# Seven-product form for the last eight hidden tiles of the second down projection, with sums of eight weight blocks made ahead

## The chip, the cores and the metric

The kernel runs on one core of one Trainium2 chip. The metric is the device time of one execution in microseconds (us), as the median of three runs. The engines of a core work side by side: TensorE (PE in the profile, its weight loads as PEld), VectorE (DVE), ScalarE (ACT), GpSimd (POOL), and SyncE (SP), whose queue issues nearly all transfers of this kernel.

## The reference

One layer of a diffusion backbone on 512 latent tokens and 256 context tokens of width 1024, all in float32: a half-step SwiGLU feed-forward stage, a token mixer (latent attention and a gated MLP, side by side), and a second half-step feed-forward stage. Each stage is modulated by a condition vector. The parts that matter here:

```python
def swiglu(h, w1, w3, w2):
    return (jax.nn.silu(h @ w1) * (h @ w3)) @ w2      # D_MODEL 1024, D_FF 2816

x = ffn_sublayer(x, ..., ffn1_w1, ffn1_w3, ffn1_w2)   # latent; the context likewise
proj = modulate(rms_norm(x, norm2_w), ...) @ w_in     # input projection of the mixer
x = x + mx[5] * token_mix(...)
x = ffn_sublayer(x, mx[6], mx[7], mx[8], norm3_w, ffn2_w1, ffn2_w3, ffn2_w2)   # returns x
```

The output is the latent stream, 512 x 1024.

## The kernel before

**Layout.** Activations lie with the channels on the 128 partitions and the tokens along the free dimension. The 2816 hidden channels of a feed-forward stage are 22 tiles of 128 (f = 0 to 21), the 1024 model channels are 8 tiles (dt or k).

**Precision.** Every float32 operand is held as a pair of rounded tensors, high and low: ACT casts the high part (`oph`, `gh`), DVE subtracts it from the source for the low part (`opl`, `gl`). A product is three matmuls: high by high, high by low, low by high (`mm3`). `Stream.operand` makes such a pair from 512 columns of a loaded weight.

**Second feed-forward stage, up.** Tiles 0 to 3 are done plainly. From tile 4 on, class `Winograd` treats tile f of w1 and w3, four channel tiles in and 256 + 256 tokens as a two by two block product, in seven block products instead of eight (Strassen's scheme in Winograd's form). One product (`prod`) is 12 matmuls of 128 x 128 by 256 columns. The weight block of a tile is one load of 1 MB (`block`, four parts of 512 columns); four sums of these parts are made by four POOL instructions per tile (`prep`, `block_sums`, `third`; results in `s` or in place). So a tile needs seven pairs, four of them from sums. The seven products run in an order that allows tile f + 1 to be opened before tile f ends (`open`, `unit`); the evacuations of PSUM are short generators that `Flow.slot` plays between products.

**Second feed-forward stage, down.** `CHUNKS2 = [4, 4, 4, 4, 2, 4]`: after units 4, 8, 12, 16 and 18 `down_flow` multiplies the last four, four, four, four or two finished hidden tiles with their part of w2, for each of the eight dt over all 512 tokens (matmuls of 512 columns), and adds the result to `x` by one DVE instruction per dt (`evac_lat`). The last four tiles are multiplied behind all units by `down`, which also sends each finished row of `x` to the output.

**What sets the order.** In the stages around the change each engine's instructions are kept in the order in which the program records them. `Flow` is a queue of weight pairs: it makes up to `OPS` = 5 pairs ahead of the product that uses them, during `down_flow` up to `OPS + MORE` = 9. SP issues loads in its own fixed order; a load waits there until its buffer is free, and everything behind it waits too. There are three buffers for loads of 512 KB (`raw`) and two for 1 MB (`block`), besides one in the pool `third`.

**End of the first stage and the input projection.** `last_mm(g, dt)` is the last down projection of the first stage, for the two halves g of the tokens, 16 calls of 18 matmuls. `last_ev` adds the result to `x` and squares it; `SsqAcc` sums the squares on DVE (`sqa`), splits the sum (`sqh`, `sql`) and has PE add it over the partitions (`done_split`). `norm2(g)` makes the normalised operand (`hf`, then `hh` and `hl`) for `in_k(g, k)`, the input projection, eight steps for each half. Behind it `uv_unit` and `QTile` follow: the gated MLP's projections and the query tiles, whose weights come through `raw`. `turned` and the `QTile`s share two PSUM buffers (`big`). POOL's first work there is `kpT` (a memset) and `rk`, powers needed by the queries.

## Time and profile before

| | us |
|---|---|
| median of 3 runs | 1104.32 (1104.23 to 1104.5) |
| time of the profiled execution | 1104.5 |
| its span, first to last instruction | 1102.5 |
| PE busy | 1097.5 |
| DVE busy | 892.8 |
| ACT busy | 536.5 |
| POOL busy | 310.3 |

The profiled execution took 2.0 us more than its span, and 0.2 us more than the median. PE is busy through nearly the whole span; the granted TensorE clock is 1.0. POOL works in bursts: in the two feed-forward stages it makes the weight sums, between 474 and 538 us of the span it has nothing to do. The rows on which the prediction rests stand in it. In a row of the timeline the first number is the start in the span, the second the duration; in a row of groups the last pair before the bar's end is busy time and mean ns of one.

### The profile page before, as it was taken

The numbers are of one execution on the slowest core, as the hardware profiler recorded it, in microseconds if no ns is written. First come the engines' busy times: TensorE is split into PE (matmuls) and PEld (weight loads), VectorE is DVE, ScalarE is ACT, GpSimd is POOL, SyncE is SP. The second block draws the span as 40 slices with busy tenths as digits, with TensorE's granted clock in tenths as the row PEclk, the third lists the DMA queues.
The fourth block names the chain that finished last, engine by engine and source line by source line (L and its number), as shares of the span: only waits on it lengthen the run. The fifth ranks groups of instructions, "written<-read, shape, count | busy, mean of one in ns | idle before, by whom it ended". The sixth has DMA issues, their size and how long they took to land.

```text
span 1102.5 us, 19621 instructions
## 1 busy us (share of the span) xinstructions
PE 1097.5 (100%) x7610; PEld 1052.5 (95%) x7610; DVE 892.8 (81%) x1594; ACT 536.5 (49%) x1115; POOL 310.3 (28%) x269
## 2 busy tenths in 40 slices
PE   9999999999999999999999999999999999999998
PEld 7899999999999999999998889999999989898997
DVE  5779998888878769866867899989988878787883
ACT  6545422431344214443765549986663535354450
POOL 0003303311344013400009317860014444352420
PEclk9999999999999999999999999999999999999999
DMA  9721354234334664412241310103222322424202
GB/s 354 279 60 47 120 172 139 100 137 148 106 124 151 233 201 164 149 54 93 97 132 61 102 50 21 39 21 102 91 94 89 123 78 93 137 78 132 99 21 77
DMA packets 35677, 125.95 MB, mean 114 GB/s; under 512 B 3712, under 2 KB 10624, under 8 KB 30976
## 3 DMA queue, kind: packets, MB, share of 16 engines
q1 hardware_dynamic: 35440, 124.63, 33.2%
q8 instruction: 60, 0.98, 0.4%
q14 instruction: 33, 0.27, 0.1%
q10 hardware_dynamic: 144, 0.06, 0.1%
HBM read 122.58 MB, written 2.10 MB: 113 GB/s over the span
## 4 chain that ended last, share of the span: by engine, by line
PE 96%; DMA 1%; DVE 1%; ACT 1%; POOL 0%; issue 0%; SPq 0%; ACTq 0%; POOLq 0%; DVEq 0%
PE mm L60 61%; PE one L60 20%; PE big L60 10%; PE big L616 1%; PE mm L601 1%; DMA scale<-wada 1%; PE mm L177 1%; PE mm L176 1%; PE mm L178 1%; PE mm L338 1%; DMA x<-xT 0%; PE big L608 0%; DVE sq L60 0%; POOL pe L60 0%; ACT hh L60 0%
## 5 line engine op out<-in xcount | busy, mean ns | idle before, releaser
L60 DVE TENSOR_TENSOR opl<-block,oph 128x512 fp32r<-128x512 f32 x216 | 195.4, 912 | 32.6 <-ACT oph L60 29.9
L60 POOL TENSOR_TENSOR block<-block 128x512 f32<-128x512 f32 x69 | 105.0, 1522 | 378.9 <-DVE opl L60 376.2
L60 ACT CAST oph<-block 128x512 fp32r<-128x512 f32 x216 | 132.3, 622 | 108.8 <-PE mm L60 85.5
L60 PE MATMUL mm<-gl,oph 128*128 128x256 f32 (+2 forms) x573 | 176.4, 308 | 0.0
L60 PE MATMUL mm<-gh,opl 128*128 128x256 f32 (+2 forms) x573 | 176.4, 308 | 0.0
L60 PE MATMUL mm<-gh,oph 128*128 128x256 f32 (+2 forms) x573 | 176.4, 308 | 0.0
L60 PEld LDWEIGHTS mm<-gh,oph 128*128 128x128 f32 x573 | 107.6, 188 | 5.5
L60 PEld LDWEIGHTS mm<-gh,opl 128*128 128x128 f32 x573 | 107.6, 188 | 5.4
L60 PEld LDWEIGHTS mm<-gl,oph 128*128 128x128 f32 x573 | 107.6, 188 | 5.4
L60 ACT CAST oph<-raw 128x512 fp32r<-128x512 f32 x127 | 76.0, 620 | 69.7 <-PE mm L60 44.4
L60 DVE SCALAR_TENSOR_TENSOR x<-mm,g,x 128x512 f32<-128x512 f32 (+2 forms) x136 | 78.7, 600 | 28.5 <-PE mm L60 27.9
L60 DVE TENSOR_TENSOR opl<-raw,oph 128x512 fp32r<-128x512 f32 x127 | 88.1, 710 | 15.3 <-ACT oph L60 14.0
L60 POOL TENSOR_TENSOR block<-s,block 128x512 f32<-128x512 f32 x35 | 48.3, 1379 | 123.8 <-DVE opl L60 122.3
L60 PE MATMUL mm<-hh,oph 128*128 128x384 f32 (+2 forms) x195 | 64.9, 333 | 0.0
L60 PE MATMUL mm<-hl,oph 128*128 128x384 f32 (+2 forms) x195 | 64.8, 333 | 0.0
L60 PE MATMUL mm<-hh,opl 128*128 128x384 f32 (+2 forms) x195 | 64.8, 333 | 0.0
L60 DVE SCALAR_TENSOR_TENSOR junk<-raw,cb 128x1024 bf16<-128x1024 f32 x48 | 62.1, 1308 | 0.2 <-DMA raw<-wada 0.2
L60 POOL TENSOR_TENSOR s<-block 128x512 f32<-128x512 f32 x34 | 53.7, 1579 | 11.4 <-DMA block<-wst 11.4
L60 DVE SCALAR_TENSOR_TENSOR raw<-raw,cb 128x1024 f32<-128x1024 f32 x32 | 42.1, 1322 | 8.3 <-DMA raw<-wada 8.2
L60 PE MATMUL one<-hl,oph 128*128 128x384 f32 x144 | 48.1, 334 | 0.0
L60 PE MATMUL one<-hh,oph 128*128 128x384 f32 x144 | 48.1, 334 | 0.0
L60 PE MATMUL one<-hh,opl 128*128 128x384 f32 x144 | 48.1, 334 | 0.0
(699 smaller groups left out, 3361.9 us busy)
## 6 DMA issues: line engine op xcount, KB each, us to landing
raw<-wst SPq DMA_DIRECT2D x77, 512.0 KB, 3.8
block<-wst SPq DMA_DIRECT2D x36, 1024.0 KB, 4.9
raw<-wada SPq DMA_DIRECT2D x56, 512.0 KB, 4.3
scale<-wada SPq DMA_DIRECT2D x16, 512.0 KB, 9.0
x<-xT SPq DMA_DIRECT2D x5, 512.0 KB, 6.4
raw<-wfirst SPq DMA_DIRECT2D x8, 256.0 KB, 8.8
out<-x SPq DMA_DIRECT2D x7, 256.0 KB, 2.3
raw<-wuq SPq DMA_DIRECT2D x2, 384.0 KB, 5.1
```

The costliest lines, as they stand in the source:

```text
L60: return lambda *a, **k: self.tc.keep_in_program_order(f(*a, **k))
L176: nc.tensor.matmul(out, lh, rh, start=first, stop=False, skip_group_check=more)
L177: nc.tensor.matmul(out, lh, rl, start=False, stop=False, skip_group_check=more)
L178: nc.tensor.matmul(out, ll, rh, start=False, stop=last, skip_group_check=more)
L338: pin(nc.tensor.matmul(pa[q, :P], scw[:, kt, 2 - 2 * w : 34 - 2 * w], units[d][w][:, kt * P : kt * P + P], start=w == 0 and kt < 4, stop=w ...
L601: pin(nc.tensor.matmul(o, l[:, c], r, start=k == 0 and m == 0 and w == 0, stop=k == NK - 1 and m == 2, skip_group_check=True))
L616: pin(nc.tensor.matmul(two(pbs[i]), ops[k][lo][:, i * P : i * P + P], lat(r, k), start=False, stop=k == NK - 1 and m == 2, skip_group_chec ...
```

## The change

**Down projection of tiles 14 to 21.** `CHUNKS2` becomes `[4, 4, 4, 2]`, so `down_flow` runs after units 4, 8, 12 and 14 and ends with tile 13. Tiles 14 to 21 are treated as a two by two block product like the up projection: even tiles against odd ones, model tile j against j + 4, 256 tokens against 256. This gives four more units (`unit7`, f = 22 to 25) of seven products each, with weight blocks of their own in the weight stream (`seven_units`). The combinations of hidden tiles that this form needs are made while units 14 to 21 run (`combine`): an even tile stores a difference in place of its second half, an odd one makes three differences, each split into high and low. `unit7` adds its results to `x` by five DVE instructions of 256 columns (`put`), and sends each of the four finished pieces, 128 KB, to the output.

**Sums made ahead.** For the blocks of f = 18 to 25 (the last four up units and the four new units) POOL no longer makes sums when the block arrives. `presums` loads each of these eight blocks earlier, as two halves of 512 KB, makes the four sums with four POOL additions of 128 x 256, and stores the half to device memory. Ten halves go through three buffers of a pool `stage` during `last_mm`; six go through the halves of one `block` buffer during `in_k`. `CALLS` says at which steps the next piece is recorded. Later `prep_sums` loads 1 MB of sums and 768 KB of the block itself for each of these f.

**Signs.** In the second stage the sums are written as additions in place (`neg`), with the signs moved to the evacuations; the number of instructions per unit stays. The memset of `kpT` moves to the fourth step of `in_k`.

The core of the diff:

```diff
-CHUNKS2 = [4, 4, 4, 4, 2, 4]
+CHUNKS2 = [4, 4, 4, 2]
+SEVEN2 = sum(CHUNKS2)
+SUMMED = 18
...
+    block_sums = [dram.tile([P, 2048], F32, name=f"sums{f}") for f in range(SUMMED, NF + 4)]
...
+        def prep_sums(self, f):
+            a = st.raw_pool.tile([P, 2048], F32, tag="block", bufs=BLOCKS, name=f"block_{nc.next_id()}")
+            src = wst[self.u0 // 2 + f]
+            nc.sync.dma_start(a[:, 0:1024], src[:, 0:1024])
+            pool = self.sums[f % 2]
+            t = pool.tile([P, 2048], F32, tag="block", bufs=1, name=f"s_{nc.next_id()}")
+            nc.sync.dma_start(t, block_sums[f - SUMMED])
+            nc.sync.dma_start(a[:, 1536:2048], src[:, 1536:2048])
+            q = [t_[:, j * 512 : j * 512 + 512] for t_, j in ((a, 0), (t, 3), (a, 1), (t, 0), (t, 2), (a, 3), (t, 1))]
+            self.ready = f, q
+        def wants_sums(self, f):
+            q = []
+            def first():
+                self.prep_sums(f)
+                q[:] = self.ready[1]
+                return st.operand(q[0])
+            return (first,) + tuple((lambda i=i: st.operand(q[i])) for i in range(1, 7))
...
-            if blk == "T3" and flow.size > OPS:
+            if blk == "T3" and flow.size > (OPS + 2 if self.seven and self.at >= SEVEN2 else OPS) or pause and flow.size > OPS:
                 flow.size -= 1
-            flow.slot(step or (lambda: None))
-            prod(bank, a, self.blocks[blk], self.n, first, cut)
+            flow.slot(step or (lambda: None), lambda: self.jobs and self.jobs.popleft()())
+            prod(bank, a, self.blocks[blk] if isinstance(blk, str) else blk, self.n, first, cut)
...
+                v.tensor_mul(seven_tmp[1] if self.seven and f >= SEVEN2 and f % 2 == 0 else Z, Z, u3)
+                if self.seven and f >= SEVEN2:
+                    self.jobs.extend(self.seven.combine(f, W, Z, gh, gl))
+                    return
...
+        def unit7(self, f, hd):
+            v, j = nc.vector, f - NF
+            banks, p1 = hd
+            X, Y, Z, W = (b[:, : self.n] for b in banks)
+            u2 = self.tmp("u2", self.n)
+            blocks, put, gate = self.seven.blocks, self.seven.put, self.seven.gates
+            def ev_x():
+                put(X, j, 0, gate[0], True)
+                yield
+            def ev_u2z():
+                v.tensor_sub(u2, p1, Y)
+                v.tensor_sub(Z, u2, Z)
+                yield
+                put(Z, j + 4, 1, gate[1])
+            def ev_w():
+                put(W, j + 4, 1, gate[1], True)
+                yield
+            def ev_lo():
+                v.tensor_add(W, W, u2)
+                put(W, j + 4, 0, gate[1], True)
+                yield
+            def ev_hi():
+                put(Z, j, 1, gate[0], True)
+                yield
+            x_part = (banks[0], blocks["B21"], False, ev_x())
+            self.product(banks[2], blocks["T1"], True, None, pause=j == 0)
+            last = f + 1 == self.end
+            if not last:
+                self.product(*x_part, pause=j == 0)
+            self.product(banks[1], blocks["T2"], True, ev_u2z())
+            self.product(banks[3], blocks["T3"], True, ev_w())
+            nxt = self.product(*x_part) if last else self.open(f + 1, None)
+            self.product(banks[3], blocks["T4"], False, ev_lo())
+            self.product(banks[2], blocks["B22"], False, ev_hi())
             return nxt
...
+    class Seven:
+
...
+        def combine(self, f, W, Z, gh, gl):
+            v, s = nc.vector, nc.scalar
+            t1, b12, t2 = seven_tmp
+            t3 = b12
+            hi = lambda o, a: s.copy(o, a)
+            lo = lambda o, a, h: v.tensor_sub(o, a, h.bitcast(F32))
+            gh, gl = gh[:, 256:512], gl[:, 256:512]
+            if f % 2 == 0:
+                v.tensor_sub(t1, b12, W)
+                hi(gh, t1)
+                return [lambda: lo(gl, t1, gh)]
+            h, l = zip(*self.parts((f - SEVEN2) // 2))
+            for n, a, b in zip(("T2", "T3", "T4"), h, l):
+                for p, t in zip(self.blocks[n], (a, b)):
+                    p.tiles.append(t)
+            v.tensor_sub(t2, Z, t1)
+            hi(h[0], t2)
+            v.tensor_sub(t3, Z, b12)
+            def second():
+                lo(l[0], t2, h[0])
+                hi(h[1], t3)
+                v.tensor_sub(t1, t2, W)
+            def third():
+                lo(l[1], t3, h[1])
+                hi(h[2], t1)
+            def fourth():
+                lo(l[2], t1, h[2])
+                hi(gh, Z)
+            return [second, third, fourth, lambda: lo(gl, Z, gh)]
+        def put(self, pt, dt, g, gate, whole=False):
+            o = x[:, dt, g * 384 : g * 384 + 256]
+            nc.vector.scalar_tensor_tensor(o, pt, gate[:, dt : dt + 1], o, ALU.mult, ALU.add)
+            if whole:
+                self.out(dt, g)
...
+    stage = fctx.enter_context(tc.tile_pool(name="stage", bufs=3))
+    quarters = lambda t: t.rearrange("p (q h c) -> p h q c", q=4, h=2)
+    AHEAD, CALLS = 10, (0, 1, 2, 4, 5, 6, 7, 8, 9, 10, 12, 13, 14)
+    def presums():
+        staged, m = {}, 2 * len(block_sums)
+        def load(n, t=None):
+            if t is None:
+                t = stage.tile([P, 4, 256], F32, tag="quarters", name=f"quarters_{n}")
+            staged[n] = t
+            nc.sync.dma_start(t, quarters(wst[U_UP2 // 2 + SUMMED + n // 2])[:, n % 2])
+        def store(n):
+            nc.sync.dma_start(quarters(block_sums[n // 2])[:, n % 2], staged.pop(n))
+        def add(n):
+            q = [staged[n][:, i, :] for i in range(4)]
+            for o, a in ((3, 2), (2, 0), (0, 3), (1, 0)):
+                nc.gpsimd.tensor_add(q[o], q[o], q[a])
+        load(0)
+        load(1)
+        yield
+        for n in range(AHEAD):
+            if n:
+                store(n - 1)
+                if n + 1 < AHEAD:
+                    load(n + 1)
+            add(n)
+            yield
+        store(AHEAD - 1)
+        if m > AHEAD:
+            late = [st.raw_pool.tile([P, 2048], F32, tag="block", bufs=BLOCKS, name=f"late{i}") for i in range(2)][1]
+            late = [late[:, i : i + 1024].rearrange("p (q c) -> p q c", q=4) for i in (0, 1024)]
+            for n in range(AHEAD, min(AHEAD + 2, m)):
+                load(n, late[n % 2])
+        yield
+        for n in range(AHEAD, m):
+            add(n)
+            if AHEAD < n < m - 1:
+                load(n + 1, late[(n + 1) % 2])
+            yield
+            store(n)
+            yield
+    presum = presums()
+    next(presum)
...
+        n = 8 * g + dt
+        if n * AHEAD // 16 != (n - 1) * AHEAD // 16:
+            next(presum, None)
...
-    nc.gpsimd.memset(kpT[64:P], 0.0)
...
+        if k in CALLS:
+            next(presum, None)
+        if k == 3:
+            nc.gpsimd.memset(kpT[64:P], 0.0)
...
+        if NK + k in CALLS:
+            next(presum, None)
...
-    last2 = (starts2[-1], CHUNKS2[-1], U_DN2 + starts2[-1])
-    down(*last2, [(0, 512)], ev3, range(NK - 1), lastu)
-    down(*last2, [(0, 256), (256, 256)], ev_half, range(NK - 1, NK), lastu)
...
```

**How the instructions stand.** Three places. First the queue of SP behind the input projection; `block` and `raw` are the weight buffers, `late` the halves of one `block` buffer, `sums` the sums in device memory. Before:

```order
L129 DMA block_10345<-wst 128x2048
L137 DMA raw_7007<-wst 128x1024
L1441 DMA raw_7092<-wuq 128x768
L1441 DMA raw_7097<-wuq 128x768
L137 DMA raw_7144<-wst 128x1024
L129 DMA block_10462<-wst 128x2048
L137 DMA raw_7209<-wst 128x1024
L137 DMA raw_7224<-wst 128x1024
```

And with the change, from the store of the fourth of the six late halves on:

```order
L1358 DMA sums_66<-late_6875 512x1x256
L1355 DMA late_6875<-wst 128x4x256
L149 DMA raw_7266<-wst 128x1024
L1358 DMA sums_67<-late_6875 512x1x256
L141 DMA block_10467<-wst 128x2048
L1358 DMA sums_67<-late_6875 512x1x256
L149 DMA raw_7331<-wst 128x1024
L141 DMA block_10613<-wst 128x2048
L149 DMA raw_7346<-wst 128x1024
```

The loads `raw_7144`, `raw_7209` and `raw_7224` of before are `raw_7266`, `raw_7331` and `raw_7346` now. The last two stand behind the last stores of sums, and the third behind a block of 1 MB as well, which goes into the buffer that these stores empty.

Second, POOL from the last weight sums of the first stage to the queries. Before:

```order
L60 TENSOR_TENSOR block_5849<-s_5851_5852,block_5849 128x512
L60 TENSOR_TENSOR block_5849<-block_5849 128x512
L60 MEMSET kpT 64x768
L60 TENSOR_TENSOR rk<-vk,nhalf 128x6
L60 TENSOR_TENSOR m_7206<-m_7206,nhalf 128x8
```

And with the change, from the ninth staged half on:

```order
L62 TENSOR_TENSOR quarters_6664<-quarters_6664 128x256 x4
L62 TENSOR_TENSOR quarters_6712<-quarters_6712 128x256 x4
L62 TENSOR_TENSOR late_6875<-late_6875 128x256 x4
L62 MEMSET kpT 64x768
L62 TENSOR_TENSOR late_6875<-late_6875 128x256 x20
L62 TENSOR_TENSOR rk<-vk,nhalf 128x6
```

64 additions now stand where POOL had only the memset, 24 of them in `late`, and `rk` stands behind all of them.

Third, DVE at the end of unit 19, an odd tile (`one` and `mm` are PSUM banks, `u`, `sl`, `p` its temporaries, `c` the temporaries of `combine`, `m2h` and `m2l` the pairs that it makes). Before:

```order
L60 TENSOR_TENSOR one_13670<-one_13670,u_13859_13860 128x256
L60 TENSOR_TENSOR one_13670<-one_13670,sl_13864 128x256
L60 TENSOR_TENSOR opl_14002<-block_13772,oph_14000 128x512
L60 TENSOR_TENSOR gl_13868<-one_13670,gh_13866 128x256
L60 TENSOR_TENSOR opl_14032<-block_13953,oph_14030 128x512
L60 TENSOR_TENSOR one_13672<-one_13672,u_13861_13862 128x256
L60 TENSOR_TENSOR gl_13868<-one_13672,gh_13866 128x256
```

And with the change:

```order
L62 TENSOR_TENSOR gl_13832<-one_13749,gh_13830 128x256
L62 TENSOR_TENSOR opl_14004<-s_13780,oph_14002 128x512
L62 TENSOR_TENSOR one_13751<-one_13751,u_13825_13826 128x256
L62 TENSOR_TENSOR c_10559<-one_13751,c_10557 128x256
L62 TENSOR_TENSOR c_10558<-one_13751,c_10558 128x256
L62 TENSOR_TENSOR m2l_10550<-c_10559,m2h_10549 128x256
L62 TENSOR_TENSOR c_10557<-c_10559,one_13749 128x256
L62 TENSOR_TENSOR opl_14030<-s_13948,oph_14028 128x512
L62 TENSOR_TENSOR m2l_10552<-c_10558,m2h_10551 128x256
```

Two differences, a third one and their low parts now stand between the product of the two halves and the next weight pairs; the low part of the tile itself (`gl_13832` from `one_13751`) follows seven rows further down.

123 lines of the change are left out of this document (90 added, 33 removed).

## The prediction

> **What bounds the kernel now.** I read the page's busy times first, then who waits for whom on PE, then the chain of waits.
>
> ```profile
> span 1102.5 us, 19621 instructions
> PE 1097.5 (100%) x7610; PEld 1052.5 (95%) x7610; DVE 892.8 (81%) x1594; ACT 536.5 (49%) x1115; POOL 310.3 (28%) x269
> PE 96%; DMA 1%; DVE 1%; ACT 1%; POOL 0%; issue 0%; SPq 0%; ACTq 0%; POOLq 0%; DVEq 0%
> PE mm L296 <- DVE epsc L231: 1.0, 1, 1.0
> PE big L608 <- ACT hh L60: 0.4, 1, 0.4
> PE mm L338 <- DMA scale<-wada: 0.2, 1, 0.2
> ```
>
> The last three rows are all the waits of PE in the whole execution: 1.6 us, all at the start. So the time is the sum of the matmuls, and whatever is taken off PE shows in full, as long as no other engine becomes late. The question is which of the others has room for the added work, and where. That is read stage by stage, from deadlines: when PE takes a thing, and when it was ready.
>
> **The change part by part.** *Matmuls.* The chain of waits has these pieces in the second feed-forward stage:
>
> ```profile
> 1036.54 13.65 PE mm L60 x75
> 1050.19 5.46 PE one L60 x48
> ```
>
> The 48 of the second row have 256 columns: 5.46 / 48 = 113.75 ns each. The 75 of the first are a down projection of two tiles, 45 of 512 columns and six halves of 256, and two up products, 24 of 256. (13.65 - 30 x 0.11375) / 45 = 227.5 ns for 512 columns, twice the other. Removed: 8 tiles x 8 dt x 3 = 192 of 512 columns, 43.7 us. Added: 4 units x 7 products x 12 = 336 of 256 columns, 38.2 us. That is **-5.5 us**. The gain is gone if one of the 336 costs 43.7 / 336 = 130 ns.
>
> The Trainium skill ("TensorE: Matmul & The Clock Gate", section "Back-to-back issue gap") speaks against this: it gives a sustained 81 ns for 128 columns and 131 ns for 512, so that short matmuls are dear. By it, with an estimated 98 ns for 256 columns on the line between, the 192 would cost 25.2 us and the 336 32.9 us, 7.7 us slower. The two rows above have this kernel's own matmuls, and they are proportional to the columns.
>
> *End of the program.* The last thing on the path is an addition of 256 columns into `x` behind the last product, then a transfer of 128 KB. With the change it is the same pair. 0, between -0.2 and +0.3.
>
> ```profile
> 1099.47 0.48 DVE L406 SCALAR_TENSOR_TENSOR x<-mm,g,x 128x256 f32<-128x256 f32 x1 [0.95 <-PE mm L178]
> ```
>
> *VectorE in the second stage.* First the load per unit, from the busy times by stretch (columns: PE, PEld, DVE, ACT, POOL, clock, DMA) and the groups by shape:
>
> ```profile
> 960.00:970.00 10.00, 10.00 (x90) 10.00 (x89) 7.85 (x11) 4.44 (x9) 5.91 (x4) 1.00 0.13 56
> 970.00:979.00 9.00, 9.00 (x82) 9.00 (x81) 7.90 (x13) 5.16 (x12) 4.68 (x3) 1.00 0.34 117
> 979.00:995.00 16.00, 16.00 (x144) 16.00 (x143) 14.36 (x24) 8.59 (x21) 7.19 (x5) 1.00 0.20 67
> L60 DVE TENSOR_TENSOR opl<-block,oph 128x512 fp32r<-128x512 f32 x77 | 78.5, 1027 | 8.2 <-ACT oph L60 6.7
> L60 DVE TENSOR_TENSOR opl<-raw,oph 128x512 fp32r<-128x512 f32 x27 | 18.1, 686 | 1.3 <-ACT oph L60 0.6
> L60 DVE TENSOR_TENSOR one<-one,u 128x256 f32<-128x256 f32 x21 | 8.9, 426 | 5.3 <-PE one L60 4.6 <-ACT one L60 0.4
> ```
>
> A unit takes PE 84 x 0.11375 = 9.55 us. DVE is busy 30.1 of the 35 us here, 8.2 us per unit. `combine` adds seven DVE instructions per two units (one difference for the even tile, three differences and three low parts for the odd), 7 x 0.426 / 2 = 1.5 us per unit: 9.7 of 9.55 us in units 14 to 17, 0.6 us too much over the four, up to 1.5 with waits on POOL. The reserve covers it: two pairs more than the usual five are kept from unit 14 on, 2.7 us of PE. From unit 18 on POOL makes no sums, and an `opl` costs 686 instead of 1027 ns: 8.2 + 1.5 - 7 x 0.34 = 7.3 us. A `unit7` has seven `opl` and eight instructions of 256 columns, at most 0.48 each: 8.6 us. ACT has room everywhere (5.2 of 9). I take **+0.1**, between 0 and 1.5; without the reserve it would be 0.6.
>
> The loads for these units are 1.75 MB each. At 4.9 us per MB even one after the other that is 8.6 of 9.55 us, and there are two buffers of each kind. 0.
>
> ```profile
> block<-wst SPq DMA_DIRECT2D x36, 1024.0 KB, 4.9
> ```
>
> *POOL and VectorE at once.* Here is what POOL's new 64 additions can do to DVE, from the timeline:
>
> ```profile
> 1042.85 1.30 POOL L60 TENSOR_TENSOR block<-block 128x512 f32<-128x512 f32 x1
> 1045.49 1.29 POOL L60 TENSOR_TENSOR block<-s,block 128x512 f32<-128x512 f32 x1 [1.34 <-DVE opl L60]
> 1042.74 1.40 DVE L60 SCALAR_TENSOR_TENSOR x<-mm,g,x 128x512 f32<-128x512 f32 x2
> 1045.92 1.41 DVE L60 TENSOR_TENSOR opl<-block,oph 128x512 fp32r<-128x512 f32 x1
> 585.76 0.74 POOL L60 TENSOR_TENSOR ta<-qn,cosw 128x256 f32<-128x256 f32 x1
> ```
>
> The fourth row's `opl` starts during the second row's addition and ends 0.55 us after it: it waited for the whole addition. The third row reads PSUM and runs at full speed beside the first. So a DVE instruction with both inputs in SBUF waits for the addition in progress, on average half of its 0.74 us, 0.37 us; four additions for one half block take 3.0 us.
>
> *First sum of squares.* With DVE's low part of the sum late, PE stops in its order.
>
> ```profile
> 515.14 0.56 DVE L60 TENSOR_TENSOR sql<-sqa,sqh 128x384 fp32r<-128x384 f32 x1 [0.58 <-ACT sqh L60]
> 516.29 0.33 PE L60 MATMUL mm<-sql,ones 128*128 128x384 f32 x1
> ```
>
> Room: 516.29 - 515.70 = 0.6 us. It and two additions ahead of it have both inputs in SBUF, 3 x 0.37 = 1.1, and POOL works some two thirds of this time: 0.7 - 0.6, **+0.2**, between 0 and 1.6 (3 x 0.74 - 0.6).
>
> *Second normalisation.* The next chain runs through `sql`, the root and the first `hl` to the second half of the input projection.
>
> ```profile
> 541.00 0.56 DVE L60 TENSOR_TENSOR sql<-sqa,sqh 128x384 fp32r<-128x384 f32 x1 [0.58 <-ACT sqh L60]
> 547.93 0.56 DVE L60 TENSOR_TENSOR hl<-hf,hh 128x384 fp32r<-128x384 f32 x1 [0.66 <-ACT hh L60]
> 551.30 0.33 PE L60 MATMUL mm<-hl,oph 128*128 128x384 f32 x1
> 536.23 0.33 SPq L129 DMA_DIRECT2D block<-wst  x1
> ```
>
> Room: 551.30 - 548.49 = 2.8 us. The late halves go into the buffer that the load of the last row waited for, so halves 10 and 11 land from 540.0 on (3.8 us each, row below) and are added until 546. Eight DVE instructions with both inputs in SBUF lie in that chain: 3.0 us late, 0.2 over the room. Halves 12 and 13 follow while the later steps run with no room left. **+0.9**, between 0 and 3. The Trainium skill ("SBUF — State Buffer", section "SBUF: two separate sides") says the lock falls on any DVE instruction with two SBUF inputs; then two steps of the root wait too, which no row shows, and this would be 1.6.
>
> *Second query tile.* SP and POOL now have the late halves in their queues ahead of the weights for the gated MLP.
>
> ```profile
> raw<-wst SPq DMA_DIRECT2D x77, 512.0 KB, 3.8
> x<-xT SPq DMA_DIRECT2D x5, 512.0 KB, 6.4
> out<-x SPq DMA_DIRECT2D x7, 256.0 KB, 2.3
> out<-x SPq DMA_DIRECT2D x2, 128.0 KB, 1.7
> 569.21 81.02 SPq L137 DMA_DIRECT2D raw<-wst  x15
> 576.01 0.62 ACT L60 CAST oph<-raw 128x512 fp32r<-128x512 f32 x1 [1.11 <-DMA raw<-wst]
> 577.93 0.36 DVE L60 TENSOR_TENSOR kpe<-big,kpe 128x192 f32<-128x192 f32 x1 [0.17 <-ACT kpe L60]
> 579.88 2.08 PE big L60 x12
> ```
>
> A store of 512 KB I estimate at 2.3 + 2 x 0.6 = 3.5 us, from the two stores shown. Half 11 lands 540.4, is added by 546.0, stored by 549.5; half 13 loaded by 553.3, added 556.3, stored 559.8; half 15 loaded 563.6, added 566.6, stored 570.1. Only then does the block of 1 MB go out, and behind it `raw_7346`, which lands between 574 and 577. Before, this load was the one that ACT waited for until 576.01. Behind that cast stand the copies that empty the bank of the second query tile (until 578.29), which PE takes at 579.88: room 1.6 us. Six transfers and three rounds of additions that wait for DVE are likely 3 us longer than this sum; less 0.6 to 1.6 of room, **+0.8**, between 0 and 15 (all transfers at the 6.4 us of the second row: half 15 is stored at 586.6, the weights land at 593).
>
> Of the rest: the moved memset has nobody waiting; the early halves share SP with loads of weights that PE needs 3 us or more after they are ready.
>
> *The sum:* 1104.5 - 5.5 + 0.1 + 0.2 + 0.9 + 0.8 = 1101.0 by the profiled execution, which is 0.2 above the median: **1100.8**.
>
> **The rivals.** *All added work hides*: DVE catches up in its idle places (0.3 us per step of the normalisation) and the stores are quick. 1104.3 - 5.5 = 1098.8. For it: PE never waits now. Against: the rooms of 0.6 and 1.6 us. *Half the gain goes at the two joints*: normalisation +2.2, query tile +2, squares +0.3: 1103.3, within 0.2%. *Slower: the late halves hold the weights.* Place: SP's queue before `raw_7346`. Price: 15 us of stall at 6.4 us per transfer, 1104.3 - 5.5 + 15 = 1114; it costs from a landing at 577.6 on, and turns the sign from 583 on, which is one more microsecond on each of the six transfers than the likely sum has. For it: pieces of 1 KB, as in the load of 6.4 us, and reads and writes at once; against: that load ran beside the opening rush. *The matmuls are not cheaper*: above 130 ns for 256 columns, as the skill's figures would have it, 1112 by them; the row of 113.75 ns leaves it 1 in 100. That the change does not do what it says would show as 192 matmuls of 512 columns remaining; the instruction order has them gone.
>
> **How the numbers follow.** Forecast (1099.6 to 1102.1) 0.37, all hidden 0.25, half the gain gone 0.24, slower 0.13, matmuls 0.01. What this kernel's measurement can tell from no change is about 0.2%, 2.2 us: faster is below 1102.1. So faster 0.37 + 0.25 = 0.62, same 0.24, slower 0.14. The range reaches from 1098.4 (everything hidden, tail -0.2) to 1104.8, which takes in most of the third case and leaves the slow ones out.
>
> **What would show it.** The groups by shape: 336 more matmuls of 256 columns at 113 to 114 ns apart. PE's list of waits: new entries for DVE `sql` at 515, `hl` at 551, and the bank of the query tile at 580, with the sizes above; none in units 14 to 25. On POOL, additions of 0.7 us, and the last of them before 567. Wrong would be: a wait of PE in units 14 to 21 (VectorE has become the bound there), loads of sums that land late, or a cast of `raw_7346` after 583.

## The result, and the profile after

The changed kernel took 1118.09 us (median of 4 runs, 1114.36 to 1118.47) against 1104.28 before (1104.23 to 1104.50): a ratio of 1.0117, 95% interval 1.0101 to 1.0133. It is slower, by 13.8 us, and outside the predicted range. The profiled execution was the quickest of the four, 1114.36 us.

The page of the changed kernel, its span and busy times:

```profile
span 1112.6 us, 20109 instructions
PE 1099.3 (99%) x7739; PEld 1058.1 (95%) x7739; DVE 922.1 (83%) x1649; ACT 547.5 (49%) x1144; POOL 341.4 (31%) x317
```

Six rows of PE's list of waits in the same execution, none of them in the list before (us in total, times, longest):

```profile
PE big L62 <- DVE kpe L62: 2.8, 1, 2.8
PE big L62 <- POOL late L62: 1.4, 1, 1.4
PE mm L62 <- DVE sql L62: 0.9, 2, 0.7
PE big L62 <- DVE opl L62: 0.8, 1, 0.8
PE mm L62 <- ACT sqh L62: 0.8, 1, 0.8
PE mm L62 <- DVE u L62: 0.8, 1, 0.8
```

Two things are to be seen. PE, whose list added up to 1.6 us before, now waits 9.3 (the six rows, 0.2 in one row more, and the 1.6 of before). And its busy time has gone up by 1.8 us, although it has 5.5 us less of matmuls: some matmuls have become slower. The granted clock tells which. Five rows of a table by stretches of 3.41 us (columns: PE, PEld, DVE, ACT, POOL, granted clock, DMA):

```profile
514.99:518.40 3.41, 1.90 (x10) 1.31 (x9) 2.64 (x5) 0.87 (x2) 3.25 (x4) 1.00 1.04 397
518.40:521.82 3.42, 3.42 (x12) 3.42 (x12) 1.81 (x4) 0.99 (x2) 1.54 (x3) 0.51 0.83 270
521.82:525.23 3.41, 3.41 (x21) 3.41 (x21) 2.65 (x4) 0.88 (x2) 1.91 (x3) 0.99 1.01 320
573.00:576.42 3.42, 3.42 (x11) 2.65 (x10) 2.15 (x4) 2.49 (x6) 2.97 (x4) 0.51 1.02 330
590.07:593.49 3.42, 2.86 (x9) 2.86 (x10) 2.69 (x10) 1.16 (x3) 3.42 (x4) 0.51 0.09 13
```

In the first row PE has only 1.90 us of work: it waits twice for the sum of squares. In the whole next stretch the clock is halved, in the third it is back. The same happens from 573.00 and from 590.07. The borders are whole multiples of 3.413 us apart (518.40 + 16 x 3.413 = 573.0, + 5 more = 590.1).

Set against each other, the start of the same matmul in the two timelines gives the account of the profiled execution. It is 0.3 us ahead from the first 10 us on. It loses 1.95 us at the first sum of squares and 1.6 in the slow stretch behind it; 0.9 at 543 (a wait for an `opl` of the input projection); 0.5 at the second sum of squares; 1.55 at 571 (the sums of squares of the query; the list puts this wait down to POOL's late additions) and 1.6 in the slow stretch; 2.95 at the second query tile and 1.35 in the slow stretch: 12.1 us in all up to 594. The second feed-forward stage takes 2.7 off, the end adds 0.7. 12.1 - 2.7 + 0.7 = 10.1; the spans differ by 10.1. For the largest of these, the first matmul of the second query tile before and after (timelines of the two kernels):

```profile
579.72 0.33 PE L60 MATMUL big<-wqh,cqh 128*128 128x384 f32 x1
```

```profile
590.63 0.69 PE L62 MATMUL big<-wqh,cqh 128*128 128x384 f32 x1 [2.78 <-DVE kpe L62]
```

What it waited for stands in the chain of waits of the changed kernel: the late halves, one behind the other. (Transfers and the last cast; the rows of the additions between them are left out.)

```profile
539.37 3.76 DMA late<-wst
552.23 6.33 DMA sums<-late
558.58 3.63 DMA late<-wst
566.19 3.28 DMA sums<-late
569.48 3.66 DMA late<-wst
576.47 4.50 DMA sums<-late
581.42 6.80 DMA raw<-wst
588.30 0.63 ACT oph L62
```

A load waits for the store of the half whose place it takes, and behind the last store in SP's queue stand a block of 1 MB and the weights of the gated MLP (`raw`). Behind their cast stand the copies that empty the bank which the query tile needs. Between a load and its store stand four additions, and these are slow too, as are VectorE's instructions beside them. The groups by shape from 505 to 590 us, before and after:

```profile
L60 DVE TENSOR_TENSOR hl<-hf,hh 128x384 fp32r<-128x384 f32 x16 | 8.9, 555 | 4.5 <-ACT hh L60 4.5
L60 DVE TENSOR_TENSOR sqa<-sqa,sq 128x384 f32<-128x384 f32 x11 | 6.1, 550 | 0.3 <-ACT sq L60 0.2
```

```profile
L62 DVE TENSOR_TENSOR hl<-hf,hh 128x384 fp32r<-128x384 f32 x16 | 13.4, 841 | 1.6 <-ACT hh L62 1.6
L62 DVE TENSOR_TENSOR sqa<-sqa,sq 128x384 f32<-128x384 f32 x11 | 7.2, 657 | 0.2 <-ACT sq L62 0.2
L62 POOL TENSOR_TENSOR quarters<-quarters 128x256 f32<-128x256 f32 x26 | 23.8, 920 | 7.1 <-DMA quarters<-wst 5.5
L62 POOL TENSOR_TENSOR late<-late 128x256 f32<-128x256 f32 x24 | 20.7, 864 | 19.7 <-DMA late<-wst 18.2
```

`hl` takes 841 in place of 555 ns, and an addition on POOL 864 to 920, where the same shape took 740 before (`ta`, in the prediction). That the two engines hold each other up is the reading; the run without additions tests it for VectorE.

### The profile page after: what moved, and what is told of

It reads as the page before. It is cut to its first block, busy times and chain, and to the rows that moved or that the text cites. A ratio compares the mean times of both kernels' runs of the same rounds, so it can differ in the third digit from the quotient of the medians.

```text
span 1112.6 us, 20109 instructions
## 1 busy us (share of the span) xinstructions
PE 1099.3 (99%) x7739; PEld 1058.1 (95%) x7739; DVE 922.1 (83%) x1649; ACT 547.5 (49%) x1144; POOL 341.4 (31%) x317
## 4 chain that ended last, share of the span: by engine, by line
PE 87%; DMA 5%; DVE 3%; POOL 2%; ACT 1%; issue 1%; SPq 0%; POOLq 0%; ACTq 0%; DVEq 0%
PE mm L62 55%; PE one L62 21%; PE big L62 9%; DMA raw<-wst 2%; DMA sums<-late 1%; POOL late L62 1%; PE big L630 1%; PE mm L615 1%; DMA late<-wst 1%; DMA scale<-wada 1%; DVE opl L62 1%; PE mm L352 1%; DMA x<-xT 0%; DVE x L62 0%; DVE one L62 0%
## 5 line engine op out<-in xcount | busy, mean ns | idle before, releaser
L62 DVE TENSOR_TENSOR opl<-block,oph 128x512 fp32r<-128x512 f32 x216 | 190.4, 888 | 29.1 <-ACT oph L62 26.7
L62 POOL TENSOR_TENSOR block<-block 128x512 f32<-128x512 f32 x61 | 91.6, 1502 | 348.0 <-DVE opl L62 345.6
L62 ACT CAST oph<-block 128x512 fp32r<-128x512 f32 x216 | 131.8, 621 | 97.2 <-PE mm L62 80.4
L62 PE MATMUL mm<-gh,opl 128*128 128x256 f32 (+2 forms) x564 | 171.2, 304 | 0.0
L62 PE MATMUL mm<-gh,oph 128*128 128x256 f32 (+2 forms) x564 | 171.2, 304 | 0.0
L62 PE MATMUL mm<-gl,oph 128*128 128x256 f32 (+2 forms) x564 | 171.2, 304 | 0.0
L62 PEld LDWEIGHTS mm<-gh,oph 128*128 128x128 f32 x564 | 106.5, 189 | 4.6 <-DVE c L62 0.4
L62 PEld LDWEIGHTS mm<-gh,opl 128*128 128x128 f32 x564 | 106.4, 189 | 4.3
L62 PEld LDWEIGHTS mm<-gl,oph 128*128 128x128 f32 x564 | 106.4, 189 | 4.2
L62 ACT CAST oph<-raw 128x512 fp32r<-128x512 f32 x119 | 70.9, 619 | 71.6 <-PE mm L62 41.3
L62 DVE TENSOR_TENSOR opl<-raw,oph 128x512 fp32r<-128x512 f32 x119 | 84.1, 723 | 19.5 <-ACT oph L62 18.6
L62 DVE SCALAR_TENSOR_TENSOR x<-mm,g,x 128x512 f32<-128x512 f32 (+2 forms) x132 | 74.5, 586 | 21.2 <-PE mm L62 20.9
L62 POOL TENSOR_TENSOR block<-s,block 128x512 f32<-128x512 f32 x31 | 42.3, 1365 | 121.0 <-DVE opl L62 120.7
L62 PE MATMUL mm<-hh,oph 128*128 128x384 f32 (+2 forms) x195 | 64.9, 333 | 0.0
L62 PE MATMUL mm<-hh,opl 128*128 128x384 f32 (+2 forms) x195 | 64.9, 333 | 0.0
L62 PE MATMUL mm<-hl,oph 128*128 128x384 f32 (+2 forms) x195 | 64.8, 333 | 0.0
L62 DVE SCALAR_TENSOR_TENSOR junk<-raw,cb 128x1024 bf16<-128x1024 f32 x48 | 62.1, 1308 | 0.5 <-DMA raw<-wada 0.5
L62 ACT CAST oph<-s 128x512 fp32r<-128x512 f32 x64 | 39.4, 621 | 36.2 <-PE mm L62 22.5
L62 POOL TENSOR_TENSOR s<-block 128x512 f32<-128x512 f32 x30 | 48.1, 1604 | 10.0 <-DMA block<-wst 10.0
L62 DVE SCALAR_TENSOR_TENSOR raw<-raw,cb 128x1024 f32<-128x1024 f32 x32 | 42.2, 1323 | 7.2 <-DMA raw<-wada 7.1
L62 PE MATMUL one<-hl,oph 128*128 128x384 f32 x144 | 48.1, 334 | 0.0
L62 PE MATMUL one<-hh,oph 128*128 128x384 f32 x144 | 48.1, 334 | 0.0
```

Of the source, the lines that this page charges most:

```text
L62: return lambda *a, **k: self.tc.keep_in_program_order(f(*a, **k))
```

## The experiments

The theory was: all the loss is made by the sums ahead of 820 us, by POOL's additions against VectorE and by the row of late halves, each wait with the slow clock behind it; the second stage nets a small gain. The rivals: the seven-product form itself is too dear for VectorE; the transfers alone are the cause; the cause is something else in the change.

| kernel | median us | its own before |
|---|---|---|
| the change, again | 1118.65 | 1104.47 |
| sums made, nobody uses them | 1119.99 | 1104.47 |
| no sums ahead | 1117.90 | 1104.47 |
| sums of five blocks | 1112.53 | 1104.47 |
| additions left out | 1104.36 | 1104.19 |
| late halves in places of their own | 1110.96 | 1104.19 |
| six halves in the first stage | 1111.27 | 1104.19 |
| twelve halves in the first stage | 1134.11 | 1104.19 |
| pause of three / of five instructions | 1105.23 / 1107.76 | 1104.24 |
| sums by accumulating transfers, 1st / 2nd / 3rd form | 1176.24 / 1131.63 / 1103.91 | 1104.24 / 1104.13 / 1104.41 |

**The change again.**

> The changed kernel once more, unchanged, for a second profile, since its first profiled execution (1114.4 us) lies 3.7 us under the other three. Theory (the sums made ahead cost 12 us between 510 and 600 us of the span, the second feed-forward stage gives about 2.5 us of net gain): 1114 to 1118.5, and where it is above 1114.4 the difference lies between 510 and 600 us. Rival (the spread comes from VectorE in the second feed-forward stage): the difference lies behind 980 us.

1118.65 us (1116.33 to 1120.18), just over the theory's upper end; the profiled execution took 1117.81. Rows of its list of PE's waits:

```profile
PE big L62 <- DVE kpe L62: 7.4, 1, 7.4
PE mm L62 <- ACT oph L62: 1.7, 1, 1.7
PE big L62 <- DVE opl L62: 1.1, 1, 1.1
PE mm L62 <- DVE u L62: 0.8, 1, 0.8
```

The wait at the query tile is 7.4 in place of 2.8 us, and a new one of 1.7 for the weights ahead of it; the wait in the second stage is the same 0.8. By the starts of the same matmuls all of the 3.5 us between the executions arises ahead of 600 us. Up to 576 the second execution is even 4.9 us ahead, since its clock stays whole there and the wait at 571 is missing; at the row of late halves it then loses 8.3.

**Sums made, but not used.** To the kernel before, the diff adds `presums` and its calls in `last_mm` and `in_k`:

```diff
+    presum = presums()
...
+        if n * AHEAD // 16 != (n - 1) * AHEAD // 16:
+            next(presum, None)
...
```

> The kernel before, with the loads, the 64 additions and the stores of the sums put in at the same steps, and nobody who uses the sums: down projection and weight sums in the second stage as before. Theory (the whole loss is made by the sums, in the normalisation, the key projection and the query tile): 1104.3 + 12.3 = 1116.5, up to 1120, with the same three groups of PE waits (515 to 518, 543 to 548, 570 to 591). Rival (the seven-product form itself costs the time): 1104 to 1107.

1119.99 us: 15.5 over before, and PE waits at the same places (4.3 for `kpe`, 1.5 for `oph`, 1.1 for `opl`, 0.8 and 0.6 at the first sum of squares). The sums cost this by themselves. The change, with the new form on top, is 1.3 us below.

**No sums ahead.**

```diff
-SUMMED = 18
+SUMMED = 26
```

> The change without sums made ahead: POOL makes the sums of all units and of the four new ones when the block arrives. Theory: nothing is lost before 820 us; -5.5 on PE, and VectorE, which waits for POOL's additions, needs 9.7 us per unit in units 14 to 21 against 9.55 of PE and up to 11 in the new ones: 1.2 to 5 us back, so 1100 to 1104. Rival (the form itself costs more than it saves, VectorE sets the pace from unit 14 on): 1106 or more. Rival (the loss upstream has another cause than the sums): 1110 or more.

1117.90 us, no wait between 30 and 980 us. The first rival's figure came out: the waits are in units 15 to 25.

```profile
PE mm L62 <- DVE u L62: 6.0, 3, 2.3
PE mm L62 <- ACT u L62: 1.9, 2, 1.3
PE mm L62 <- DVE x L62: 1.9, 2, 1.4
```

Here the spacing of the matmuls behind 826 us adds up to 18.7 us more than their number asks for, 2.3 in the change. So the form without sums ahead is nearly as bad as the sums alone (13.4 us against 15.5): VectorE cannot pay for both the combinations and POOL's additions at the same time. I had bounded this at 5 us by VectorE's load, and forgotten that the waits come in pieces, here of 0.5 to 2.3 us, and can slow the clock, here twice.

**Five blocks** (`SUMMED = 21`, so no late halves).

> The change with sums of five blocks (f = 21 to 25) in place of eight: the ten halves go through the three staging buffers during the last down projection as in the change, and there are no late halves. Theory (of the 12.3 us some 8 come from the late halves: waits at 543, 570, 591 and the slowed clock behind them; 3.3 to 4 from the staged ones): 1114.4 - 8 = 1106, between 1104 and 1108. Rival (POOL's additions as such are the cause, so that ten of sixteen halves cost ten sixteenths): 1110.

1112.53 us: above theory (1104 to 1108) and rival (1110) both. Ahead of 820 us only 2.9 us are lost (0.9 at 516, 2.0 up to 543), so the late halves were 9 of 12 us, as the theory had it. But three more blocks summed beside the units cost 7.3 us there (9.6 in place of 2.3 in the spacing), which the theory had not counted.

**Additions left out.**

```diff
-            q = [staged[n][:, i, :] for i in range(4)]
-            for o, a in ((3, 2), (2, 0), (0, 3), (1, 0)):
-                nc.gpsimd.tensor_add(q[o], q[o], q[a])
+            pass
```

The kernel leaves out the sums of these eight blocks, so its output is not the layer's; its time is what counts here.

> The change with all 64 additions of the sums left out, so that the sums stored are the plain blocks (this leaves out part of the computation); all loads and stores stand as they were. Theory A (POOL's additions are the cause: VectorE waits for them at 515 and 541, and they stand in the row of load, addition and store of the late halves): nothing lost at 515 and 541, the last late half stored about 562, no wait at the query tile; what is left is the second stage's 2.4 and the end's 0.7: 1104.4 - 5.5 + 3.1 = 1102 to 1103.5. Theory B (the transfers alone make the weights late): a wait at the query tile of over 2 us stays, 1108 or more.

1104.36 us (1102.67 to 1107.21 in 10 runs): 14 us less than the change with all its transfers in place. In the profile no wait at 516 or 543 is left, and `hl` takes 556 ns. At the query tile

```profile
PE big L62 <- DVE kpe L62: 0.5, 1, 0.5
PE mm L62 <- ACT oph L62: 0.3, 1, 0.3
```

stay; there this execution, one of the longer ones with 1106.1 us, is 2.3 us behind the kernel before. So theory A holds, and the transfers have a small share. The median is 1 us above what I expected. The share of the transfers shows ahead of the first sum of squares too:

```profile
501.30 0.62 ACT L62 CAST block_l<-raw 128x512 fp32r<-128x512 f32 x1 [1.72 <-DMA raw<-wst]
516.25 0.56 DVE L62 TENSOR_TENSOR sql<-sqa,sqh 128x384 fp32r<-128x384 f32 x1 [0.58 <-ACT sqh L62]
```

Weights that share SP's queue with the halves land late, two casts wait 1.7 and 2.4 us for them, and `sql` ends at 516.81, 1.1 us later than before (515.70), with no addition on POOL. In the change it ends at 517.88: the other 1.1 comes with the additions.

**Late halves in places of their own.**

```diff
-            late = [st.raw_pool.tile([P, 2048], F32, tag="block", bufs=BLOCKS, name=f"late{i}") for i in range(2)][1]
+            free = [t.rearrange(r)[:, :2048] for t, r in ((qn, "p a b c -> p (a b c)"), (ut, "p a c -> p (a c)"))]
```

> The change with the six late halves in four places of 512 KB of tensors that are used only later (qn, ut), in place of the two halves of one block buffer; all transfers, additions and their order on each queue stay. Theory A (the loads of the late halves wait for stores, and the 1 MB block and the weights behind it wait for the buffer): the last half is added by 567 and stored by 571, the weights of the query tile land before 577, no wait there; left are some 3 us at 515 to 542, the second stage's 2.4 and the end's 0.7: 1104.4 - 5.5 + 6 = 1105, 1104 to 1107. Theory B (the lock by POOL's additions delays the copies): the waits at 571 and 590 stay, 1112 or more.

1110.96 us, 7 below the change and 4 above the upper end of what theory A gave (1107). The wait at the query tile is gone, as expected. But now the additions run together from 545 to 570, in the second normalisation, and new waits stand in PE's list:

```profile
PE mm L62 <- DVE hl L62: 1.8, 6, 0.9
```

In the groups by shape from 505 to 590 us `hl` is at its slowest:

```profile
L62 DVE TENSOR_TENSOR hl<-hf,hh 128x384 fp32r<-128x384 f32 x16 | 15.1, 955 | 0.7 <-ACT hh L62 0.7
```

Both causes are real: the row of late halves, and the additions against VectorE. Taking the first away gives part of it to the second.

**Halves in the first stage.** Six, then twelve of the halves are recorded with the up units of the first stage, through `st.raw()`:

```diff
+        if i == 1 and f - 1 in UNITS:
+            add(UNITS.index(f - 1))
+        if i == 3:
+            if f - 1 in UNITS:
+                store(UNITS.index(f - 1))
+            if f in UNITS:
+                load(UNITS.index(f), st.raw().rearrange("p (q c) -> p q c", q=4))
...
```

> The change with the six late halves made during the first feed-forward stage, one each in units 8, 12, 13, 14, 18 and 20, through one of the three buffers for loads of 512 KB; ten halves stay in the last down projection. Theory (the late halves cost 9 us, VectorE has a fifth of its time free in the first stage): 1104.4 - 5.5 + 2.9 + 3.1 = 1105, 1104 to 1107. Rival (the buffer taken makes the first stage's loads late, or VectorE has no room there): a wait of PE between 200 and 480, 1108 or more.

> The change with twelve of the sixteen halves made during the first feed-forward stage, one each in units 5, 7, 8, 9, 11 to 15, 17, 18 and 20, and four in the first seven steps of the last down projection, so that POOL has none left when the first sum of squares is split. Theory (the upstream loss goes as a whole): 1104.4 - 5.5 + 2.4 + 0.7 = 1102, 1101.5 to 1103.5, a little faster than before. Rival (the first stage becomes late): PE waits between 120 and 480, 1106 or more.

1111.27 and 1134.11 us: the rivals. With six, PE waits between 350 and 480 us, up to 1.6 at a time. With twelve:

```profile
PE mm L62 <- DVE gl L62: 7.1, 4, 3.2
PE one L62 <- DVE u L62: 4.7, 2, 3.3
PE mm L62 <- DVE u L62: 4.5, 3, 1.9
PE mm L62 <- ACT u L62: 3.9, 1, 3.9
```

VectorE is 82 to 84% busy in that stage before (100 to 480 us), but its free share does not lie where the copies of PSUM (`u`) come due. Whether the lock or the taken buffer weighs more there was not separated.

**A pause of known length.** In the kernel before, the low part of the first sum of squares is computed several times:

```diff
-            sums[0].lo()
+            for _ in range(4):
+                sums[0].lo()
```

> The kernel before, in which VectorE computes the low part of the first sum of squares four times in place of once (the same values into the same tile): 3 x 0.56 = 1.7 us later, less the room of 0.6: PE waits 1.1 us in one piece at 516.3 and nowhere else. Theory (a wait of PE costs more than itself once it fills enough of a window of 3.41 us that runs on its own count; in the change 0.82, 1.10 and 1.26 us in a window did not, 1.35 and 1.52 did): 1104.3 + 1.1 = 1105.4, all matmuls at full speed. Rival (every wait near 1 us slows the clock): 1107.

> The same with six times in place of one: 5 x 0.56 = 2.8 us later, PE waits 2.2 us in one piece at 516.3. Theory: the window behind it runs at half the clock, 3.41 us in which a 384-column matmul takes 0.32 in place of 0.173 us, 1.6 us more on top: 1104.3 + 2.2 + 1.6 = 1108.1; if the wait falls across the border of two windows, 1106.5. Rival (a wait costs what it lasts): 1106.5 always.

1105.23 and 1107.76 us, as the theory had it (1105.4, 1108.1). From the timelines of PE, first with four, then with six computations:

```profile
517.47 0.45 PE L60 MATMUL mm<-sql,ones 128*128 128x384 f32 x1 [1.08 <-DVE sql L60]
517.75 0.34 PE L60 MATMUL mm<-gh,oph 128*128 128x384 f32 x1
519.33 0.33 PE L60 MATMUL mm<-gh,oph 128*128 128x384 f32 x1
```

```profile
518.55 0.45 PE L60 MATMUL mm<-sql,ones 128*128 128x384 f32 x1 [2.27 <-DVE sql L60]
519.08 0.52 PE L60 MATMUL mm<-gl,oph 128*128 128x384 f32 x1
521.96 0.51 PE L60 MATMUL mm<-gl,oph 128*128 128x384 f32 x1
```

Behind a wait of 1.08 us the nine steps from 517.75 to 519.33 are 0.176 us each; behind one of 2.27 us the nine steps from 519.08 to 521.96 are 0.32 us each. The wait of 2.27 us costs 3.5 us in the medians. The single runs with six computations show the border that the expectation named: six of the ten took 1107.68 to 1108.25 us at a mean granted clock of 0.998, four took 1106.35 to 1106.69 at 1.000. The same wait costs about 2.4 us where the clock stays whole and 3.6 where it does not. With four computations the clock is 1.000 in all ten.

**Sums by accumulating transfers.** The last experiments leave the additions to DMA: the block is copied within device memory, then its parts are added there by transfers that POOL issues. The two lines are from the third form.

```diff
...
+            copies.append(lambda d=d, src=src: pin(nc.sync.dma_start(d, src)))
...
+            adds7.append(lambda o=o, a=a: [pin(nc.nc.gpsimd.dma_start(p[o], p[a], accum_op=ALU.add)) for p in q])
```

> The change with its sums made by transfers alone: each of the eight blocks is copied within device memory, and four accumulating transfers of 256 KB (in two parts each, issued by POOL) add its parts, one step at a time during units 5 to 20 of the first stage; no additions on POOL and no staging buffers. Theory (the loss is POOL's additions against VectorE and the row of late halves; the second stage as in the change): 1104.3 - 5.5 + 2.4 + 0.7 = 1102, 1101.5 to 1103, faster than both. Rival A (the added 40 MB of transfers delay the loads of the first stage): PE waits between 100 and 480, 1106 or more. Rival B (POOL, which issues them and waits for each, is late with the first stage's own sums): PE waits there too, with DVE opl behind POOL in the list.

1176.24 us. My copies had been moved to the front of SP's queue, ahead of the first loads (PE waits 19.8 us for `scale`), and POOL, which waits for each accumulation, was late with the first stage's own sums (rival B; 36.4 us for ACT's `u`).

> The sums by transfers once more, with what made the first try slow taken away: the eight copies stand in SP's order at units 5 to 12 of the first stage (in the first try they were at the very front, ahead of the loads of the start), the accumulating transfers run in pairs on two halves of a block, and POOL issues them where it makes no sums of its own: fifteen pairs in the three down projections of the first stage, fourteen in the last one, three in the input projection. Theory (the waits of the first try were the copies at the start and POOL's own sums behind the accumulations; a pair takes about 4.5 us, 32 of them 145 us in 160 us of such stretches): nothing is lost before 820 us, 1104.3 - 5.5 + 2.4 + 0.7 = 1102, 1101.5 to 1103. Rival (transfers of weights and accumulations delay each other in the down projections, or POOL is not done when the key projection needs its memset): 1105 or more, with PE waits between 135 and 420 or near 570.

1131.63 us, with one main cause in the profiled execution: POOL was not through when the key projection needed its memset, since a pair takes 6.9 us (`PE big L62 <- POOL kpT L62: 19.6, 1, 19.6`). Nothing was lost ahead of 566 us; waits between 630 and 650 us cost some 3 us more.

> The sums by accumulating transfers, as in the try before, whose only loss ahead of 600 us was one wait of 19.6 us for the memset that stood behind the accumulations on POOL (a pair took 6.9 us there, not 4.5). Now nine pairs, not seventeen, stand ahead of that memset (487 + 9 x 6.9 = 549, needed at 566), and eight are issued behind 747 us, where POOL has nothing to do until 820 (8 x 6.9 = 55). Theory (the loss of the change is POOL's additions and the row of late halves, and the second stage nets 2.4): 1104.2 - 5.5 + 2.4 + 0.7 = 1101.8, 1101.2 to 1103. Rival (something else of the change costs time): 1104 or more, with no wait for POOL.

In the profiled execution, 1102.12 us, these are all the waits of PE:

```profile
PE mm L310 <- DVE epsc L245: 1.0, 1, 1.0
PE mm L62 <- DVE u L62: 0.6, 1, 0.6
PE big L622 <- ACT hh L62: 0.4, 1, 0.4
PE mm L497 <- DVE sq L62: 0.2, 1, 0.2
PE mm L62 <- DVE x L62: 0.2, 1, 0.2
PE mm L352 <- DMA scale<-wada: 0.2, 1, 0.2
```

All eight blocks have their sums from transfers, and nothing is lost ahead of 820 us. The span is 1100.3 us, 2.2 below before: the second stage's net gain, by itself, as the theory had it. But the median of 11 runs is 1103.91 (1101.77 to 1107.89), ratio 1.0001 (0.9990 to 1.0012): no difference from before that can be measured, and the theory's range (up to 1103) is missed. Two more profiles show what varies.

> The kernel with accumulating transfers unchanged, for a second profile. Theory A (a transfer takes longer in some executions, and what waits behind it on POOL or SP comes late ahead of 830 us): where the time is over 1103.5, the excess stands ahead of 830 us in PE's waits, at one or two places, with the slowed clock behind. Theory B (VectorE in the second stage): the excess stands behind 990 us.

> The same, a third profile; the same two theories. If both lie under 1103 the question stays open.

One took 1101.98 us, the other 1107.27. Theory A has part of the difference: between 395 and 435 us, where accumulations run beside a down projection of the first stage, and in the unit behind it, 4.0 us are lost (waits of 1.3 and 1.1 among them), and 3.5 are left at 830. The rest, 1.9, is neither: from 1010 to 1065 us the matmuls of 256 columns lie 117.8 ns apart, not 113.4. In the windows from 1020 to 1040 us, first of the execution of 1107.27 us and then of that of 1101.98, PE is busy all the time, at the same granted clock, with fewer matmuls:

```profile
1020.00:1040.00 20.00, 20.00 (x172) 20.00 (x172) 18.47 (x40) 12.54 (x31) 0.00 (x0) 1.00 0.59 161
```

```profile
1020.00:1040.00 20.00, 20.00 (x179) 20.00 (x178) 18.52 (x40) 13.15 (x32) 0.00 (x0) 1.00 0.73 184
```

What slows them is not known.

## Why the prediction was wrong

Three steps failed. The second query tile was sized by quiet rows (+0.8; measured 2.95 to 7.6). A wait of PE was priced at its own length, with no term for the slow clock behind it (4.6 us in the profiled execution). And the early halves' place in SP's queue was put at nothing, where it used up a room that the forecast counted on.

**The matmuls** (-5.5): right. 256 columns take 113.4 ns in units 14 to 21 and about 116 in the new units; the difference is counted under VectorE. The rival that they are not cheaper was false. (The 130 ns in it is the price at which the gain is gone; the estimate that it leans on was 98 ns.)

**The end** (0, from -0.2 to +0.3): +0.7. From the start of the last matmul to the end of the span it is 4.1 us (1112.6 - 1108.5), before 3.3 (1102.5 - 1099.2). "It is the same pair" was right: from the last matmul's start to the landing of the last transfer it is 2.54 us, before 2.55. The 0.7 lies behind that landing, in the program's closing instructions (1.50 us, before 0.83; 1.20 in the third form with accumulating transfers). Why these took longer is open.

**VectorE in the second stage** (+0.1, up to 1.5): 2.8 given back of 5.5, 0.9 at the wait for `u` in the first units with combinations, 0.5 at the first new unit, the rest in slower matmuls and small gaps. The place was right, the size above my bound. The stage nets 2.7 us. A wait of PE there was named as a sign of being wrong, and it came.

**First sum of squares** (+0.2, up to 1.6): 1.95, above the upper end. `sql` took 1.11 in place of 0.56 us, the two `sqa` ahead of it 0.96 and 0.82 in place of 0.55: 1.2 us for the three, where I had taken 0.7. That part was right in kind. But the room of 0.6 was not there: in the run without additions the late weights alone make `sql` 1.1 us late. The step that failed is "the early halves share SP with loads of weights that PE needs 3 us or more after they are ready"; their casts and VectorE's work on them came late, and the sums of squares stand behind these.

**Second normalisation** (+0.9, up to 3): 1.4, but 0.9 of it at an `opl` of the input projection at 543, which I had not looked at.

**Second query tile** (+0.8, up to 15): 2.95 in the profile of the change and 7.6 in the second one; the other runs of the change, like the second profile, took 1118. The sum of quiet rows said: half 11 stored 549.5, half 13 stored 559.8, half 15 stored 570.1. The chain shows 558.6, 569.5 and 581.0. Most of the 11 us come in the first round: the halves landed 3 us later (543.1), POOL took 8.9 us for eight additions, a memset and the gaps between them, not 6, and the store took 6.3 us, not 3.5. The cast behind `raw_7346` began at 588.3, past the 583 named as a sign of being wrong. My price of an addition was one measured where VectorE was not competing. The step from the sum to the term was loose as well: 3 us less 0.6 to 1.6 of room is 1.4 to 2.4, not 0.8. Of the rivals, "the late halves hold the weights" had the place and the sign, and I gave it 0.13; its 1114 was built from a wait of 15 us at one place, and that the profiled execution took 1114.36 is luck: its loss came about at several places, with 2.95 us at this one.

**What was missing altogether:** a price for a wait beyond its own length. I had let each joint cost what it is late. Three stretches of 3.41 us at half the clock stand behind waits of the change: 4.6 us, in the profiled execution more than the wait at the query tile itself. The query statistics at 571 (1.55 us), where the squares `sqq` take up to 0.95 in place of 0.43 us beside POOL's additions, had no term either.

The Trainium skill, "SBUF — State Buffer", section "SBUF: two separate sides", says that a DVE instruction with two SBUF inputs shares a port with GpSimd's reads; the trace agrees, with 841 to 955 in place of 555 ns for `hl` and 864 to 920 in place of 740 for POOL's additions. I had it, and priced it at half an addition, 0.37 us. On the average of the 16 `hl` it was 0.29, and 0.40 where additions ran back to back, so the price was not far off; what it is worth at each joint was.

## What to carry to other kernels

Where one engine is busy through the whole span, price each new wait of it as the wait plus the slow stretch that may follow it (1.3 to 1.6 us here), and look for it at every joint, not at two. Work on POOL is not free because POOL is idle: additions there cost VectorE, and are themselves slower beside it. A row of load, work and store through few buffers is as long as the sum of its loaded times, not of the quiet ones, and whatever stands behind it in the same queue inherits the delay.

## What the runs showed of the hardware

A wait of TensorE can slow the stretch behind it. The slow stretches are 3.41 us long, or several of these in a row, and keep their own time through the execution. Waits of 1.35 (571 us), 1.52 (0.82 + 0.70 at 516) and 2.27 us in one stretch were followed by half the clock in the next (0.51 granted, 0.32 us for 384 columns in place of 0.173); 0.82, 0.73 (what one stretch held of the pause of 1.08) and, without sums ahead, 1.26 us were not. The length of the wait alone does not decide it. With the late halves in places of their own 1.16 us at 574 was enough, in a stretch that also held matmuls of one column; 1.70 us at 578 in the second profile of the change and 1.54 at 1010 without sums ahead, each within one stretch, left the clock whole. What else counts was not tested. The Trainium skill, "TensorE: Matmul & The Clock Gate", section "Part 1: The HAM clock gate", has the free-running window of 3.4 us and the half rate, and the trace agrees; it puts the return to half rate at a whole idle window, and here part of one was enough, at 571 us 1.35 of 3.41.

An accumulating transfer of 128 KB within device memory kept POOL about 3.5 us in the first of these kernels (median to landing; 3.8 and 4.0 in the other two): 0.8 to issue it and the rest in waiting for it. The copy of one block within device memory took 16.8 us there, beside the loads of the start, and a load of 1 MB 4.9; copies of half a block, 512 KB, took 6.5 and 6.8 us in the other two, a load of that size 4.0 and 4.2.
